# A gated branch in half units and a delta-rule pair projected early, in the first block of a two-block kernel

## The chip, the cores and the metric

One core of a Trainium2 chip runs the whole program in one launch. The metric is device time in microseconds (us), the median of the runs. Lower is better.

## The reference

Two transformer blocks act on 512 latent positions and 256 context positions of width 1024, batch 1, in float32. The change lies in the first block. There the normed and modulated input is projected by `w_in`, and the result feeds three branches:

- a pooling branch (4 windows);
- a delta-rule branch (RWKV, 6 heads of 64, two directions). A state is carried over the positions, context first, then latent positions:

```python
sa = einsum('bhvk,bhk->bhv', S, kk_t)
S = S * w_t - sa[..., None] * (kk_t * a_t) + v_t[..., None] * k_t
y = einsum('bhvk,bhk->bhv', S, r_t)
```

- a gated branch (HGRN, 6 heads of 64, two directions), a gated linear recurrence computed chunk by chunk, with `g` the running sum of the log of the forget gate within a chunk:

```python
o = (q * exp(g)) @ S + tril(sum_k q_t k_s exp(g_t - g_s)) @ i
S = exp(g_last) * S + (k * exp(g_last - g)).T @ i
```

The branches are concatenated, gated by a silu of another part of the projection, projected by `w_out`, and added to the input. The second block (a chunked delta net, attention, two feed-forward parts) isn't touched.

## The kernel before

The kernel is written in a tile language. Python traces the operations in program order; at build time a scheduler lays out each engine's fixed order, in which an operation that is ready may be put before earlier ones that are not. Tiles with the same tag share a number of slots (`bufs`); a new tile waits until the slot's last user is done. PSUM has 8 banks, split by tag in `banks(...)`.

**Projections.** `dense` (line 267) multiplies a 1024x128 block of weights with the input. Weights come in two halves of 512 rows by DMA (`wblock`, line 256): ACT rounds them into `whi` (line 263), VectorE (DVE) takes the rest into `wlo` (line 264), and TensorE (PE) makes three products per 128 rows (line 277). Streams have weight buffers of their own: "m" for the delta rule, gates and pooling, "f" for the gated branch, "a" for the `ada` vectors (line 307: 16 transfers each and matmuls of 128x256, line 318).

**The branch stage** is the second half of `block1` (from line 448), some 70 to 850 us of the trace. The PSUM banks are `mm` 2 (projections of stream "m" and the preparation), `rsc` 2 and `rch` 1 (delta rule), `mf` 2 (everything of the gated branch, its projections too) and `ma` 1 (ada). Two generators are advanced by turns in a loop of six steps (lines 472 to 481); each step also traces one of the six block-2 `ada` vectors, the first step a further one and the pooling branch.

**The delta rule** (`rwkv_pair`, line 615) goes over three pairs of heads. A pair projects k, v and r with a three-tap shift (`shift3`, line 588; eviction in lines 582 to 585), normalises keys into `kk`, and prepares decays and scaled keys (`rwkv_prep`: matmuls in line 689, tiles `tw`, `ta`, `G`, `km`, and the prepared keys BK in lines 724 and 727). Three groups of four chunks follow: `rwkv_pre` makes score matrices (line 763) and inverts triangles on DVE and PE; `rwkv_chunk` (line 914) passes the state on, chunk after chunk (lines 926 to 945; one of its matmuls is line 934); `rwkv_out` makes the output. A gate projection follows a group. After the third group a readout normalises y (lines 656 to 669).

**The gated branch** (`hgrn_pair`, line 983) has six units: three pairs of heads, two directions. A pair projects q and the values `it`; a unit projects z, from which come `g`, the keys, and the decayed keys `kd` (`hgrn_unit`, line 1042). Then six chunks are walked in order. The four latent chunks make scores at seven levels (`hgrn_levels`; 32-wide matmuls in lines 1084 to 1091), mask and sum the inner levels on DVE (1094, 1096), and copy the diagonal blocks and the outer levels into `sct` on ACT (1099 to 1104). Two matmuls a head with the state and with `sct` (1111, 1112) give the output. Between chunks the state is moved on: a transpose of `kd` on PE (1120), an ACT copy (1122), two matmuls (1125), and two DVE updates (1130) into a zeroed new tile `hS`.

Ahead of the gating at the end, `gated(j)` multiplies each branch's output with its gate on POOL and splits it (lines 484 to 491, 398, 399).

Of the kernel before, what the change touches and what calls it, by code (L numbers as in the profile page):

```python
# [49 lines left out]
def _consts():  # L50
    p = np.arange(128)
    c = {}
# [13 lines left out]
    for d in range(2):  # L66
# [9 lines left out]
        c[f"hgm{d}"] = np.concatenate(lv, 1) * 1.0  # L76
    s5, t5 = p[:, None] % 32, np.arange(32)[None]
# [120 lines left out]
class B:  # L198
    def __init__(self, ctx, tc, d, taps=()):
        self.tc, self.nc, self.d, self.taps = tc, tc.nc, d, taps  # L200
        self.ctx = ctx
        self.cst = ctx.enter_context(tc.tile_pool(name="cst", bufs=1))
        self.wp = ctx.enter_context(tc.tile_pool(name="wp", bufs=3))
        self.hp = ctx.enter_context(tc.tile_pool(name="hp", bufs=1))
        self.streams = {"m": (self.wp, 2, 2)}
        self.load_consts()
# [220 lines left out]
    def block1(self):  # L427
# [20 lines left out]
        with ExitStack() as ctx:  # L448
            ctx.enter_context(self.banks(mm=2, rsc=2, rch=1, mf=2, ma=1))
            ctx.enter_context(self.stream("f", 2, 1))  # L450
            ctx.enter_context(self.stream("a", 3, 1))
# [11 lines left out]
            self.sct = [self.f1.tile([128, 2, 128], F32, name=f"sct{a}") for a in range(2)]  # L463
            for x in self.sct:
                nc.gpsimd.memset(x, 0.0)
# [3 lines left out]
            rw = chain.from_iterable(self.rwkv_pair(p) for p in range(3))  # L469
            hg = chain.from_iterable(self.hgrn_pair(p) for p in range(3))  # L470
            next(rw)
            for n in range(6):
                for _ in range(2 - n % 2):
                    next(rw, None)
                next(hg)
                if n == 0:
                    self.ada(s, 0, d["mod_w"], 1, 2, mod[:, 16:24], self.V("mod_b", 16, 8), "a")
                    self.pool_branch()
                l, g = divmod(n, 3)
                self.ada(s, 2, d["ada_w"][l], g, 4, self.m2[l][:, 16 * g:16 * g + 16],  # L480
                         self.V("ada_b_2", 48 * l + 16 * g, 16), "a")
# [59 lines left out]
    def pool_branch(self):  # L541
        nc = self.nc
        for j in range(2):
# [23 lines left out]
            pw = self.f2.tile([128, 128], F32, tag="hkt", name="pw")  # L567
# [47 lines left out]
    def rwkv_pair(self, p):  # L615
        nc = self.nc
        k = self.f1.tile([128, NT], F32, name="rk")
        v = self.f1.tile([128, NT], F32, name="rv")
        r = self.f1.tile([128, NL], F32, name="rr")
        kk = self.f1.tile([128, NT], F32, name="rkk")  # L620
        self.shift3(5 + p, (LAT, CTX), k)
        self.shift3(8 + p, (LAT, CTX), v)
        self.shift3(2 + p, (LAT,), r, -256)
        nc.scalar.activation(kk, k, AF.Copy, scale=self.V("rwkv_k_k", p))
        sq = self.f1.tile([128, NT], F32, tag="tw", name="kksq")
        nc.gpsimd.tensor_tensor(sq, kk, kk, op=ALU.mult)
        rn = self.f1.tile([128, NT], F32, tag="G", name="kkrn")
        pieces = []
        for c0, cn in (LAT, CTX):
            o = self.mm()  # L630
            nc.tensor.matmul(o[:, :cn], self.C("bones"), sq[:, c0:c0 + cn], start=True, stop=True)
            pieces.append((rn[:, c0:c0 + cn], o[:, :cn]))
        self.rsqrt_bc(rn, pieces, 1.0, 3)
        nc.vector.tensor_tensor(kk, kk, rn, op=ALU.mult)
        pb = self.f1.tile([128, NL], F32, name="rpb")
        bk, ec = self.rwkv_prep(p, r, k, v, kk, pb)
        yield
        y = self.f1.tile([128, NL], F32, name="ry")
        st = self.f1.tile([128, 2, 64], F32, tag="rS", name="rS", bufs=8)
        nc.gpsimd.memset(st, 0.0)  # L640
        for g in range(3):
            pre = self.rwkv_pre(g, bk, v)
            sts = []
            for i in range(4):
                sts.append(st)
                st = self.rwkv_chunk(g, i, ec[:, :, 4 * g + i], pre, st)
            if g:
                self.rwkv_out(g, sts, pre, y)
            if 3 * p + g < 8:
                self.gate(3 * p + g)  # L650
            if g < 2:
                yield

        def readout():

            sq = self.f1.tile([128, NL], F32, name="rsq")
# [10 lines left out]
            if p < 2:  # L667
                nc.sync.dma_start(self.ymix[:, 2 + p], y)

        readout()  # L670

    def rwkv_prep(self, p, r, k, v, kk, pb):
# [70 lines left out]
    def rwkv_pre(self, g, bks, v):  # L743
# [49 lines left out]
        w = f1.tile([128, 8, 32], F32, tag="rw16", name="rw32")  # L793
# [28 lines left out]
    def inv8(self, c32, U):  # L822
# [29 lines left out]
        w = tl("w16", 32)  # L852
# [61 lines left out]
    def rwkv_chunk(self, g, i, ec, pre, st):  # L914
# [14 lines left out]
        xs = self.f1.tile([128, 128], F32, name="xs", bufs=2)  # L929
# [10 lines left out]
        st2 = self.f1.tile([128, 2, 64], F32, tag="rS", name="rS", bufs=8)  # L940
# [42 lines left out]
    def hgrn_pair(self, p):  # L983
        nc = self.nc
        f1, f2 = self.f1, self.f2
# [7 lines left out]
        for c0, n in ((2, 4), (0, 2)):  # L993
            tp = self.psum("mf", (128, 4, 128))
# [3 lines left out]
        oa = f1.tile([128, NL], F32, name="hoa")  # L998
        for dd in range(2):
            z = f1.tile([128, NT], F32, name="hz")  # L1000
            for (c0, cn), o in zip((LAT, CTX), self.dense(self.d["w_in"], 19 + 3 * dd + p, self.hh, self.hl, (LAT, CTX), st="f")):
                nc.scalar.copy(z[:, c0:c0 + cn], o[:, :cn])
            self.hgrn_unit(p, dd, q, it, z, oa)
            yield
# [776 lines left out]
```

## Time and profile before

| | us |
|---|---|
| median of 3 runs | 2729.93 (2725.15 to 2731.68) |
| profiled execution | 2736.78 |
| its span, first to last instruction | 2735.0 |
| PE busy in the span | 2523.7 |
| DVE busy | 1621.3 |
| ACT busy | 1276.9 |
| POOL busy | 319.3 |

PE is the matmul engine, PEld its weight loads, which overlap. A row of a window gives start and end, the length, then for PE, PEld, DVE, ACT and POOL the busy us with the number of instructions, then the mean granted clock of PE (1.00 is 2.4 GHz, 0.50 is 1.2 GHz), the share of DMA in use and GB/s. A window filtered by line or tile shows only engines that such instructions run on. Idle time of PE is length less busy time. A row of a group gives line, engine, operation, output and inputs, shapes and count, then busy us and mean ns of one, then the engine's idle time just before them and what ended it. A row of a wait reads: who waited, for whom, us in all, times, longest.

### The profile page before, as it was taken

The page shows a single profiled execution, that of the slowest core. Times are in us where ns is not written, and L with a number is a line of the kernel's source. Part 1 is how long each engine was busy: PE and PEld are TensorE (multiplying, and loading weights), DVE is VectorE, ACT ScalarE, POOL GpSimd, SP SyncE. Part 2 cuts the span into 40 slices and gives each one's busy share as a digit, 9 for nine tenths or more (in the row PEclk, how much of TensorE's full clock was granted, in tenths as well). Part 3 has the DMA queues.
Part 4 walks back from the last instruction along what each step waited for, and adds up shares of the span by engine and source line. Part 5 has one row for each costly group of instructions (what it writes and reads, how often), then busy time and mean ns, then how long its engine had stood idle before and what let it go on. Part 6 is the DMA issues. An engine that isn't in the chain of part 4 may idle for free.

```text
span 2735.0 us, 53289 instructions
## 1 busy us (share of the span) xinstructions
PE 2523.7 (92%) x21320; PEld 1990.5 (73%) x21320; DVE 1621.3 (59%) x3815; ACT 1276.9 (47%) x2840; POOL 319.3 (12%) x432
## 2 busy tenths in 40 slices
PE   7989979979877989989899999999998999999998
PEld 3655646545546777777677888888886888888888
DVE  4566574576565656777856443344463767664665
ACT  3454454545455656556434332233344555542444
POOL 0121121122112000111110110011000000010010
PEclk9999989989887999999989999999998999999999
DMA  6233432434334211111231112212231102233325
GB/s 206 77 94 118 139 98 92 125 100 134 93 104 146 72 39 32 36 41 37 65 105 47 62 63 64 63 63 66 80 105 44 32 27 95 78 100 93 100 89 157
DMA packets 159016, 231.10 MB, mean 84 GB/s; under 512 B 12976, under 2 KB 90032, under 8 KB 158768
## 3 DMA queue, kind: packets, MB, share of 16 engines
q1 hardware_dynamic: 158768, 227.70, 26.7%
q8 instruction: 167, 2.74, 0.4%
q14 instruction: 81, 0.66, 0.1%
HBM read 217.95 MB, written 9.70 MB: 83 GB/s over the span
## 4 chain that ended last, share of the span: by engine, by line
PE 47%; DVE 2%; ACT 2%; issue 1%; POOL 1%; DMA 0%; POOLq 0%; SPq 0%; DVEq 0%; ACTq 0%
PE mm L277 39%; PE ms L1735 2%; PE mt L1754 1%; PE mv L351 1%; PE mt L1748 1%; PE mm L1685 1%; PE mf L277 0%; DVE hl L423 0%; DVE ht L421 0%; POOL qr L1669 0%; ACT hh L422 0%; DMA raw<-mla_w_out 0%; ACT whi L263 0%; ACT qrh L1705 0%; PE mm L1665 0%
## 5 line engine op out<-in xcount | busy, mean ns | idle before, releaser
L264 DVE TENSOR_TENSOR wlo<-raw,whi 128x512 fp32r<-128x512 f32 (+3 forms) x560 | 391.3, 701 | 395.1 <-ACT whi L263 236.6
L263 ACT CAST whi<-raw 128x512 fp32r<-128x512 f32 (+3 forms) x560 | 331.9, 594 | 462.8 <-PE mm L277 398.9
L277 PE MATMUL mm<-hh,whi 128*128 128x512 f32 (+1 forms) x1960 | 483.8, 360 | 28.0 <-ACT hh L422 13.6
L277 PE MATMUL mm<-hl,whi 128*128 128x512 f32 (+1 forms) x1960 | 457.3, 350 | 0.0
L277 PE MATMUL mm<-hh,wlo 128*128 128x512 f32 (+1 forms) x1960 | 455.3, 350 | 0.4 <-DVE wlo L264 0.4
L277 PEld LDWEIGHTS mm<-hh,whi 128*128 128x128 f32 x1960 | 332.4, 192 | 89.7 <-ACT hh L422 21.0
L277 PEld LDWEIGHTS mm<-hl,whi 128*128 128x128 f32 x1960 | 329.7, 193 | 46.8 <-issue 3.6
L277 PEld LDWEIGHTS mm<-hh,wlo 128*128 128x128 f32 x1960 | 328.9, 193 | 45.0 <-issue 2.0
L1233 POOL TENSOR_TENSOR fc<-fc,fc 128x768 f32<-128x768 f32 (+1 forms) x44 | 69.2, 1573 | 867.9 <-DVE fc L585 625.8
L277 PE MATMUL mm<-fh,whi 128*128 128x256 f32 (+1 forms) x616 | 136.3, 340 | 1.0 <-ACT fh L398 1.0
L583 DVE SCALAR_TENSOR_TENSOR fc<-mm,vec,fc 128x511 f32<-128x511 f32 (+1 forms) x132 | 86.8, 658 | 80.7 <-ACT fc L582 80.7
L277 PE MATMUL mm<-fl,whi 128*128 128x256 f32 (+1 forms) x616 | 130.5, 330 | 0.0
L277 PE MATMUL mm<-fh,wlo 128*128 128x256 f32 (+1 forms) x616 | 129.3, 328 | 0.0
L582 ACT ACTIVATE fc<-mm,vec 128x512 f32<-128x512 f32 (+1 forms) x132 | 81.4, 617 | 97.2 <-PE mm L277 97.2
L277 PEld LDWEIGHTS mm<-fh,whi 128*128 128x128 f32 x616 | 99.8, 190 | 15.8 <-issue 3.4
L318 PE MATMUL ma<-raw,cvs 128*32 128x256 f32 x832 | 95.6, 427 | 15.3 <-DMA raw<-ada_w 10.6
L277 PE MATMUL mf<-hh,whi 128*128 128x512 f32 (+1 forms) x360 | 103.6, 387 | 6.0 <-ACT whi L263 3.4
L277 PEld LDWEIGHTS mm<-fl,whi 128*128 128x128 f32 x616 | 99.0, 190 | 11.3 <-issue 0.5
L1197 DVE SCALAR_TENSOR_TENSOR xr<-mm,m,xr 128x512 f32<-128x512 f32 (+1 forms) x112 | 66.5, 597 | 67.0 <-PE mm L277 66.8
L277 PEld LDWEIGHTS mm<-fh,wlo 128*128 128x128 f32 x616 | 98.6, 190 | 10.4
L351 PE MATMUL mv<-sq,con 128*128 128x256 f32 (+1 forms) x240 | 84.3, 452 | 12.4 <-ACT sq L355 12.0
L277 PE MATMUL mf<-hl,whi 128*128 128x512 f32 (+1 forms) x360 | 95.4, 367 | 0.0
(545 smaller groups left out, 4383.6 us busy)
## 6 DMA issues: line engine op xcount, KB each, us to landing
raw<-ada_w SPq DMA_DIRECT2D x96, 512.0 KB, 4.6
raw<-ffn_up SPq DMA_DIRECT2D x176, 256.0 KB, 2.8
raw<-ffn_down SPq DMA_DIRECT2D x96, 256.0 KB, 2.7
raw<-w_in SPq DMA_DIRECT2D x66, 256.0 KB, 2.9
raw<-ab_w_in SPq DMA_DIRECT2D x50, 256.0 KB, 2.6
raw<-ffn_down SPq DMA_DIRECT2D x48, 192.0 KB, 2.4
raw<-mod_w SPq DMA_DIRECT2D x16, 512.0 KB, 7.6
raw<-w_out SPq DMA_DIRECT2D x32, 256.0 KB, 2.9
```

Source lines behind the costliest of these rows:

```text
L263: nc.scalar.copy(hi[:, :nk], raw[:, :nk])
L264: nc.vector.tensor_tensor(lo[:, :nk], raw[:, :nk], hi[:, :nk].bitcast(F32), op=ALU.subtract)
L277: nc.tensor.matmul(o, a[:, k], b[:, k0 + k, t:e], start=(k0 == 0 and j == 0 and k == 0), stop=(k0 + n == nk and j == 2 and k == n - 1))
L318: nc.tensor.matmul(acc[32 * b:32 * b + 32, c:c + 256], s[:, k, :], t[:, b], start=(k == 0), stop=(k == 7))
L351: self.nc.tensor.matmul(v[:, :x.shape[1]], self.C("ones"), x, start=(k == 0), stop=(k == 7))
L582: nc.scalar.activation(out[:, c0:c0 + cn], o[:, :cn], AF.Copy, scale=w[1])
L583: nc.vector.scalar_tensor_tensor(out[:, c0 + 1:c0 + cn], o[:, :cn - 1], w[0], out[:, c0 + 1:c0 + cn], op0=ALU.mult, op1=ALU.add)
L1197: nc.vector.scalar_tensor_tensor(x, o[:, :cn], gcol(m, 0 if c0 else 1), x, op0=ALU.mult, op1=ALU.add)
L1233: nc.gpsimd.tensor_tensor(g, g, u, op=ALU.mult)
L1685: nc.tensor.matmul(o[:, e], a[:, k, T], b[:, k], start=(i == 0), stop=(i == 5))
L1735: nc.tensor.matmul(o[:, at:at + cn], a, b, start=(j == 0), stop=(j == 4))
L1748: nc.tensor.transpose(tp[:, j], p[:, (c0 + j) * 128:(c0 + j + 1) * 128], self.C("ident"))
```

## The change

The two generators become `rwkv_steps` and `hgrn_steps`, advanced in nine steps, one per group of the delta rule. The gated branch yields after each half of a unit (two latent chunks). All states of a unit are made at once by `hgrn_states` into a persistent tile `hS` of four states; `hgrn_prep` makes z, g and the transposed decayed keys `kt` one unit ahead. k and r of the next pair (`rwkv_load`) are traced after the second group, v (`rwkv_value`) and the preparation after the third. The mask of the diagonal blocks becomes one POOL product with a constant `b32`. PSUM tag `mf` becomes `hb`, used by the gated branch without its projections, which now use `mm`. Some buffer counts change.

```diff
-        self.streams = {"m": (self.wp, 2, 2)}
+        self.streams = {"m": (self.wp, 3, 2)}
...
-            ctx.enter_context(self.banks(mm=2, rsc=2, rch=1, mf=2, ma=1))
+            ctx.enter_context(self.banks(mm=2, rsc=2, rch=1, hb=2, ma=1))
             ctx.enter_context(self.stream("f", 2, 1))
-            ctx.enter_context(self.stream("a", 3, 1))
+            ctx.enter_context(self.stream("a", 2, 1))
...
-            for n in range(6):
-                for _ in range(2 - n % 2):
-                    next(rw, None)
-                next(hg)
+            for n in range(9):
+                next(rw, None)
+                for _ in range(1 + (n % 3 == 2)):
+                    next(hg, None)
                 if n == 0:
...
+                if n < 7:
+                    adas[n]()
...
+    def rwkv_steps(self):
+        now = self.rwkv_load(0)
+        v = self.rwkv_value(0)
+        for p in range(3):
+            bk, ec = self.rwkv_prep(p, *now, v, pb)
+            yield
...
+            for g in range(3):
+                pre = self.rwkv_pre(g, bk, v)
...
+                if g < 2:
+                    self.gate(3 * p + g)
+                    if g and p < 2:
+                        now = self.rwkv_load(p + 1)
+                    yield
+            if p < 2:
+                self.gate(3 * p + 2)
+                v = self.rwkv_value(p + 1)
...
-            sq = self.f1.tile([128, NL], F32, name="rsq")
+            sq = self.f1.tile([128, NT], F32, tag="km", name="rsq")[:, :NL]
...
-        w = f1.tile([128, 8, 32], F32, tag="rw16", name="rw32")
+        w = f1.tile([128, 8, 32], F32, tag="rc32", name="rw32")
...
-        xs = self.f1.tile([128, 128], F32, name="xs", bufs=2)
+        xs = self.f1.tile([128, 128], F32, name="xs")
...
-        st2 = self.f1.tile([128, 2, 64], F32, tag="rS", name="rS", bufs=8)
+        st2 = self.f1.tile([128, 2, 64], F32, tag="rS", name="rS", bufs=6)
...
+    def hgrn_steps(self):
+        q, it = self.hgrn_load(0)
+        prep = self.hgrn_prep(0, 0)
+        yield
+        for p in range(3):
+            oa = f1.tile([128, NL], F32, name="hoa")
+            for dd in range(2):
+                k, g, ge, kt = prep
+                self.hgrn_states(dd, ge, kt, it)
+                if dd == 0:
+                    prep = self.hgrn_prep(p, 1)
+                elif p < 2:
+                    prep = self.hgrn_prep(p + 1, 0)
+                for m in range(2):
+                    self.hgrn_chunks(dd, m, q, it, k, g, oa)
+                    if m == 0 or dd == 0:
+                        yield
...
+            if p < 2:
+                nc.sync.dma_start(self.ymix[:, 5 + p], oa)
+                q, it = self.hgrn_load(p + 1)
+            yield
...
+    def hgrn_prep(self, p, dd):
+        z = f1.tile([128, NT], F32, name="hz", bufs=2)
...
+        g = f1.tile([128, 6, 128], F32, name="hg", bufs=2)
...
+        for n0 in (0, 4):
+            n = min(4, 5 - n0)
+            tp = self.psum("hb", (128, 4, 128))
+            for n_ in range(n):
+                nc.tensor.transpose(tp[:, n_], kd[:, order[n0 + n_]], self.C("ident"))
+            nc.scalar.copy(kt[:, n0:n0 + n], tp[:, :n])
+        return z, g, ge, kt
+
+    def hgrn_states(self, dd, ge, kt, it):
+        kv = self.psum("hb", (128, 5, 64))
+        for n in range(5):
+            for h in range(2):
+                H = slice(64 * h, 64 * h + 64)
+                nc.tensor.matmul(kv[H, n], kt[:, n, H], it[:, order[n], H], start=True, stop=True)
+        ks = self.f1.tile([128, 5, 64], F32, name="hkv")
+        nc.scalar.copy(ks, kv)
+        for n in range(1, 5):
+            for h in range(2):
+                H = slice(64 * h, 64 * h + 64)
+                last = ks[H, 0] if n == 1 else self.hs[H, n - 2, H]
+                nc.vector.scalar_tensor_tensor(self.hs[H, n - 1, H], last, ge[H, order[n]:order[n] + 1], ks[H, n],
+                                               op0=ALU.mult, op1=ALU.add)
...
-                    for i in range(4):
-                        R = slice(32 * i, 32 * i + 32)
-                        nc.scalar.copy(sct[R, h, R], rd[R])
+                nc.gpsimd.tensor_tensor(sct[h].rearrange("p (i t) -> p i t", t=32),
+                                        rd.rearrange("p (o t) -> p o t", o=1).broadcast_to([128, 4, 32]),
+                                        self.C("b32").rearrange("p (i o) -> p i o", o=1).broadcast_to([128, 4, 32]), op=ALU.mult)
```

## Rows read from the trace of the kernel before

**Rows 1.** Busy time of the page: us, share of the span, instructions, by engine.

```profile
PE 2523.7 (92%) x21320; PEld 1990.5 (73%) x21320; DVE 1621.3 (59%) x3815; ACT 1276.9 (47%) x2840; POOL 319.3 (12%) x432
```

**Rows 2.** Windows of the branch stage: busy us by engine, clock, DMA share, GB/s.

```profile
187.00:240.00 53.00, 43.41 (x956) 29.06 (x956) 41.62 (x147) 33.04 (x123) 10.24 (x24) 0.81 0.28 86
...
306.00:336.00 30.00, 28.55 (x180) 21.39 (x181) 21.72 (x50) 19.51 (x47) 4.26 (x4) 1.00 0.35 111
336.00:378.00 42.00, 28.18 (x357) 14.78 (x351) 36.84 (x80) 20.53 (x51) 14.49 (x30) 0.72 0.46 148
...
434.00:473.00 39.00, 38.32 (x664) 27.89 (x662) 19.71 (x64) 18.73 (x47) 5.96 (x11) 1.00 0.31 98
473.00:552.00 79.00, 73.56 (x1286) 46.90 (x1284) 46.56 (x151) 41.57 (x152) 14.13 (x26) 0.91 0.41 128
...
566.00:608.00 42.00, 27.39 (x152) 15.54 (x152) 35.32 (x70) 22.57 (x37) 15.22 (x27) 0.75 0.35 113
...
674.00:717.00 43.00, 40.81 (x633) 29.25 (x629) 18.93 (x63) 16.21 (x43) 6.03 (x11) 0.92 0.22 73
717.00:798.00 81.00, 68.19 (x1304) 42.05 (x1300) 48.17 (x152) 44.43 (x159) 9.60 (x21) 0.89 0.40 125
...
808.00:849.00 41.00, 21.43 (x405) 12.18 (x405) 22.60 (x66) 20.33 (x86) 9.64 (x13) 0.50 0.38 123
sum 697.00, PE 595.02 PEld 381.76 DVE 421.90 ACT 352.11 POOL 131.79; mean PE 39.67 PEld 25.45 DVE 28.13 ACT 23.47 POOL 8.79
```

**Rows 3.** Windows of line 1084 alone, PE and PEld.

```profile
482.00:520.00 38.00, 5.71 (x384) 4.45 (x384) 0.89 0.55 170
```

**Rows 4.** Windows of line 934 alone, PE and PEld.

```profile
482.00:520.00 38.00, 0.00 (x0) 0.00 (x0) 0.89 0.55 170
```

**Rows 5.** Waits of PE, 70 to 850 us: total us, times, longest.

```profile
PE rsc L763 <- DVE BK L727: 18.3, 4, 7.7
PE mf L1112 <- ACT sct L1099: 11.0, 18, 2.7
PE ma L318 <- DMA raw<-ada_w: 10.6, 14, 2.8
PE mf L1111 <- ACT sct L1104: 8.6, 8, 2.2
```

**Rows 6.** Groups by line, ACT, 70 to 850 us.

```profile
L1099 ACT COPY sct<-hrd 32x32 f32<-32x32 f32 x192 | 41.1, 214 | 7.5 <-DVE hrd L1096 3.0 <-DVE rpr L847 0.6
...
L1122 ACT COPY hkt<-mf 128x128 f32<-128x128 f32 x30 | 7.5, 267 | 3.8 <-PE mf L1120 3.3
```

**Rows 7.** Groups by line, DVE, 70 to 850 us.

```profile
L1130 DVE SCALAR_TENSOR_TENSOR hS<-hS,hge,mf 64x64 f32<-64x64 f32 x60 | 16.8, 280 | 14.7 <-PE mf L1125 3.6 <-ACT hoa L1115 3.5 <-ACT hlv L1037 2.9
...
L583 DVE SCALAR_TENSOR_TENSOR rv<-mm,vec,rv 128x511 f32<-128x511 f32 (+1 forms) x6 | 3.7, 612 | 4.0 <-ACT rv L582 4.0
```

**Rows 8.** Groups by line, POOL, 70 to 850 us.

```profile
L1107 POOL TENSOR_TENSOR hqe<-hqe,hq 128x128 f32<-128x128 f32 x24 | 14.4, 602 | 72.8 <-ACT hqe L1106 60.5 <-PE ma L318 8.8 <-PE rsc L787 3.1
```

**Rows 9.** Timeline of ACT: start, length, instruction.

```profile
534.91 0.69 ACT L582 ACTIVATE rk<-mm,vec 128x512 f32<-128x512 f32 x1
```

**Rows 10.** Groups by line and shape, PE, 70 to 850 us.

```profile
L318 PE MATMUL ma<-raw,cvs 128*32 128x256 f32 x832 | 95.6, 427 | 15.3 <-DMA raw<-ada_w 10.6 <-DMA raw<-mod_w 2.9 <-ACT sct L1099 1.6
...
L277 PE MATMUL mf<-hh,whi 128*128 128x512 f32 x96 | 35.8, 463 | 0.5 <-ACT whi L263 0.5
```

**Rows 11.** DMA issues, 70 to 850 us: count, KB each, us to landing.

```profile
raw<-ada_w SPq DMA_DIRECT2D x96, 512.0 KB, 4.6
```

**Rows 12.** Timeline of POOL and DVE, 815 to 830 us.

```profile
816.18 1.27 POOL L490 TENSOR_TENSOR gb<-ga,gb 128x512 f32<-128x512 f32 x1
...
816.76 1.24 DVE L399 TENSOR_TENSOR hl<-gb,hh 128x512 fp32r<-128x512 f32 x1 [0.26 <-ACT hh L398]
...
828.88 0.68 DVE L399 TENSOR_TENSOR hl<-gb,hh 128x512 fp32r<-128x512 f32 x1
```

**Rows 13.** Windows of the matmuls into tile mf, PE alone.

```profile
434.00:473.00 39.00, 19.46 (x89) 1.00 0.31 98
```

More of the change, by code (lines that the diff above doesn't have):

```diff
@@ L76, in _consts @@
         c[f"hgm{d}"] = np.concatenate(lv, 1) * 1.0
+    c["b32"] = (p[:, None] // 32 == np.arange(4)[None]) * 1.0
     s5, t5 = p[:, None] % 32, np.arange(32)[None]
@@ L462, in block1 @@
                 nc.gpsimd.memset(a, 0.0)
-            self.sct = [self.f1.tile([128, 2, 128], F32, name=f"sct{a}") for a in range(2)]
-            for x in self.sct:
-                nc.gpsimd.memset(x, 0.0)
+            self.hs = self.f1.tile([128, 4, 128], F32, name="hS")
+            nc.gpsimd.memset(self.hs, 0.0)
             self.rwkv_lora()
@@ L566, in pool_branch @@
             nc.vector.tensor_tensor(tot, tot, u, op=ALU.subtract)
-            pw = self.f2.tile([128, 128], F32, tag="hkt", name="pw")
+            pw = self.f2.tile([128, 128], F32, tag="hqe", name="pw", bufs=1)
             nc.gpsimd.memset(pw, 0.0)
@@ L668, in readout, with rwkv_value, rwkv_load, rwkv_prep @@
                 nc.sync.dma_start(self.ymix[:, 2 + p], y)
-        readout()
-    def rwkv_prep(self, p, r, k, v, kk, pb):
+                y = self.f1.tile([128, NL], F32, name="ry")
+    def rwkv_value(self, p):
+        v = self.f1.tile([128, NT], F32, name="rv")
+        self.shift3(8 + p, (LAT, CTX), v)
+        return v
+    def rwkv_load(self, p):
+        nc = self.nc
+        k = self.f1.tile([128, NT], F32, name="rk")
+        r = self.f1.tile([128, NL], F32, name="rr")
+        kk = self.f1.tile([128, NT], F32, name="rkk")
+        self.shift3(5 + p, (LAT, CTX), k)
+        nc.scalar.activation(kk, k, AF.Copy, scale=self.V("rwkv_k_k", p))
+        sq = self.f1.tile([128, NT], F32, tag="tw", name="kksq")
+        nc.gpsimd.tensor_tensor(sq, kk, kk, op=ALU.mult)
+        rn = self.f1.tile([128, NT], F32, tag="G", name="kkrn")
+        pieces = []
+        for c0, cn in (LAT, CTX):
+            o = self.mm()
+            nc.tensor.matmul(o[:, :cn], self.C("bones"), sq[:, c0:c0 + cn], start=True, stop=True)
+            pieces.append((rn[:, c0:c0 + cn], o[:, :cn]))
+        self.rsqrt_bc(rn, pieces, 1.0, 3)
+        nc.vector.tensor_tensor(kk, kk, rn, op=ALU.mult)
+        self.shift3(2 + p, (LAT,), r, -256)
+        return r, k, kk
+    def rwkv_prep(self, p, r, k, kk, v, pb):
         nc = self.nc
@@ L997, in hgrn_pair @@
             nc.scalar.copy(it[:, c0:c0 + n], tp[:, :n])
[L998 to L1004, printed above, removed]
-        sq = f1.tile([128, NT], F32, tag="htmp", name="osq")
@@ L1006, in hgrn_pair @@
-        nc.gpsimd.tensor_tensor(sq[:, :NL], oa, oa, op=ALU.mult)
-        va = self.psum("mf")
-        nc.tensor.matmul(va, self.C("bones"), sq[:, :NL], start=True, stop=True)
-        rs = f1.tile([128, NT], F32, tag="hg", name="ors")
-        self.rsqrt_bc(rs[:, :NL], [(rs[:, :NL], va)], 1.0 / 64, 1)
-        nc.vector.scalar_tensor_tensor(oa, oa, self.V("hgrn_norm_g", p), rs[:, :NL], op0=ALU.mult, op1=ALU.mult)
-        self.last[5 + p] = oa
-        if p < 2:
-            nc.sync.dma_start(self.ymix[:, 5 + p], oa)
+        return q, it
```

234 lines of the change are left out of this document (104 added, 130 removed).

## The prediction, made before the changed kernel was run

> **What bounds the kernel now.** I read the page's busy line first: TensorE (PE) is busy for 92% of the span [rows 1], so a change to one stage can gain only where PE in that stage stands idle or runs at its lower clock. The change touches the branch stage alone, some 70 to 850 us. Next I read the windows table of that stage [rows 2]. Over 152 to 849 us PE is busy 595.0 of 697 us, so 102 us are idle. It is uneven. Two stretches, 434 to 473 and 674 to 717, in which a group of the delta rule runs beside filler, leave 0.7 and 2.2 us idle at a granted clock of 1.00 and 0.92. The idle time is in four kinds of stretch: 187 to 240 and 717 to 798 (9.6 and 12.8 us idle, each holding a unit of the gated branch), 336 to 378 and 566 to 608 (13.8 and 14.6 us; keys of the next pair are prepared and VectorE, DVE, is busy 36.8 and 35.3 of 42 us), and the end, 808 to 849 (19.6 us of 41, clock 0.50, so all of it at the lower of PE's two levels, 1.2 GHz).
>
> Third, two windows tables of one line each. The score matmuls of the gated branch come in bursts: all 384 of a unit lie within 482 to 520 [rows 3]. In the same window the delta rule's chunk matmuls stand at zero [rows 4]. So a gated unit, traced as one block, displaces a group: the group in 473 to 552 lasts 79 us and the one in 717 to 798 lasts 81, while the undisturbed ones last 39 and 43 [rows 2]. That is no loss by itself, since the displaced work is not lost, but it makes the thin stretches and leaves the last unit alone at the end.
>
> Fourth, the waits of PE within 70 to 850 us [rows 5]: for BK (line 727, the prepared keys) 18.3 us, for `sct` (the masked scores, lines 1099 and 1104) 11.0 and 8.6, for ada weights by DMA 10.6.
>
> **The change part by part.** Measured by the profiled execution, 2736.78 us around a span of 2735.0; it stands 6.85 us above the median of the runs, 2729.93.
>
> *The state chain.* Before, each of five chunks in a unit makes a transpose, an ACT copy (267 ns, [rows 6]), two matmuls and two DVE updates of 280 ns reading PSUM [rows 7], between the outputs of chunks, in the two `mf` banks that the scores and the projections also use. After, five transposes come at once, two wide ACT copies in place of five, ten matmuls into one bank, one ACT copy, and eight DVE updates in SBUF. PE's instructions are the same in number. DVE loses 12 of 60 updates (12 x 0.28 = 3.4 us), the memsets of the states go, and one of six exponentials and products of `kd` a unit. None of these lies on PE; what counts is that the score, output and state steps no longer take turns in a bank.
>
> *The score mask.* Before, four ACT copies a head put the diagonal blocks in place: 192 x 214 ns = 41.1 us of ACT [rows 6], and PE waits 11.0 + 8.6 = 19.6 us for the result. After, one POOL product of 128x128 a head, 48 in all, in front of the three other ACT copies. The nearest POOL row is `hqe`, 128x128, 602 ns [rows 8]: 48 x 0.60 = 29 us on POOL, which is busy 319 of 2735 us [rows 1], in a chain where 4 x 0.214 = 0.86 us of ACT stood. The chain gets 0.26 us shorter a head, and three copies now wait for POOL's semaphore too; behind them on ACT wait the weight casts of line 263. The wait of PE can go from 19.6 to somewhere between 10 and 25 us; I take 13.
>
> *Bursts broken up.* Units are split in two halves, one per group, and the next unit's z, g and kt are made one unit ahead. For 187 to 240 and 717 to 798: idle 9.6 + 12.8 = 22.4 us. With the score wait I take 10 of it, and 5 for the clock (0.81 and 0.89 there). **Gain 15, bounds 0 and 27.**
>
> *The end.* Unit 5's scores now lie beside the last group instead of behind it. Of 808 to 849, 19.6 us are idle, and the 21.4 us of PE work at clock 0.50 would take at best 10.7 at 1.00: 30 us at most. But the last step is thin after the change too: the ada transfers and gates are handed out by the step before or earlier, and the closing norm and gating stay. **Gain 20, bounds 5 and 30.**
>
> *k and r of the next pair ahead of the last group.* The projections themselves are PE work and move, they don't go: 306 to 336 has PE busy 28.6 of 30 us. What can go is the start of the preparation behind them. 336 to 378 and 566 to 608 hold 28.4 us idle, and at clocks 0.72 and 0.75 half or more of 84 us at the lower level, worth up to 15 us of PE's 55.6. Two things hold it back: preparation is bound by DVE there, and its `km` now shares a slot with the readout's `rsq`, so that half waits for the readout. Also, the order is already looked ahead at compile time: for pair 2, k is evicted at 534.9 us, before the readout that ends that pair near 552 [rows 9]. **Gain 15 of 43, bounds 0 and 35.**
>
> *One pair of banks for all projections.* The gated projections lose `mf` and join the delta rule's in `mm` (two banks), handed out in program order. Before, 12 calls of the gated branch filled PE from banks of their own (96 matmuls of one of six forms alone take 35.8 us, [rows 10]). Now each waits for the eviction of the call before: an ACT operation and two DVE operations of 612 ns each where it is a shift [rows 7], some 1.8 us. 12 x 1.8 = 22 us if nothing covers it. PE's cover is the ada matmuls (95.6 us in all, [rows 10]), scores and groups. If that cover is gone, it's 22 us; if a bank is held for a value tile that isn't free, more (the slow rival). **Loss 5, bounds 0 and 22.**
>
> *ada with two buffers in place of three, weights with three in place of two.* Bytes and transfers are equal. An ada transfer lands in 4.6 us [rows 11]; one fewer in flight makes PE's 10.6 us wait at most half as long again, and SP, an in-order queue, stands longer before an ada issue with weight loads behind it. The third weight buffer lets one load go ahead of it. **Loss 4, bounds -3 and 10.**
>
> *POOL against DVE.* When POOL multiplied 512 columns (816.18, 1.27 us), the DVE subtraction that began in it took 1.24 us; the same one alone takes 0.68 [rows 12]. So a POOL product can hold a DVE operation until it ends. 48 new products of 0.6 us: up to 29 us on DVE, mostly where DVE has just finished the mask's reduction and isn't critical. **Loss 1, bounds 0 and 15.** The Trainium skill, SBUF — State Buffer, section Who interferes with whom, has this as a lock: a DVE instruction with two SBUF inputs contends with a POOL instruction that reads SBUF, and issue order decides who blocks. The trace agrees with its 1.24 against 0.68 us; by that rule, taken for every product, the loss term would be the 15 and not the 1.
>
> The state buffers from 8 to 6, `xs` from 2 to 1 and the shared `w` slot cost nothing as long as a group's chunks follow one another through the state, as they do; bound 3 us. The first steps and everything after 850 us stay.
>
> Sum: 15 + 20 + 15 - 5 - 4 - 1 = 40 us. 2736.8 - 40 = 2696.8 for a profiled execution, and 2730 - 40 = **2690** for the median.
>
> **Rivals.** *A: the units really interleave.* Then bursts no longer displace groups, and idle and clock losses go over the whole stage: 15 + 20 + 15 become 27 + 30 + 35 = 92, less 10: 2648. For it: groups without a unit run in 39 to 43 us with PE full [rows 2]. Against: what is moved only displaces filler, since PE is at 85% in the stage.
>
> *B: nothing to move.* The look-ahead already does it [rows 9], PE's work is unchanged, and gains of 10 are eaten by bank and buffer waits: 2722 to 2738.
>
> *C: the lock.* Every POOL product holds DVE in stretches where DVE is full: the loss of 15 in place of 1, and the score chain gains nothing (7 us less): 2730 - 40 + 14 + 7 = 2711. The page named above is its rule. Against it: 602 ns on POOL [rows 8] replace 856 on ACT, and PE waits for the sum of them.
>
> *D: slower, by the shared banks.* `rv` has one buffer, freed when the last group has transposed the old values. A value projection that runs early holds both `mm` banks until then; gates, the gated z and the next pair's preparation queue behind it, and PE has only ada, with two buffers. Each of the 12 gated calls then uncovers some 5 us: 60 - 40 = 20 us slower, 2750. It decides from 40 / 12 = 3.3 us per call. For it: in 434 to 473 half of PE's time, 19.46 of 39 us, is projections into just that second pair of banks [rows 13]. Against: 306 to 336 runs three projections back to back in the two `mm` banks with 1.5 us idle [rows 2].
>
> **How the numbers follow.** Forecast 0.42 (2675 to 2705), A 0.20, C 0.11, B 0.10, D 0.17. A measurement of this kernel tells 0.3%, 8 us, from no change. Faster: forecast, A and C, 0.73; same: B, 0.10; slower: D, 0.17. The time is the likeliest case's, 2690. The range: A's low end with the bounds' best sum is 2640; at the top it takes in C, B and the near half of D, 2742. About 2 in 10 lie outside, half of them in D.
>
> **What would show it.** Right: the window of the last unit's scores overlaps the last group's chunk matmuls, and the low-clock stretch at the end is under 25 us (41 before); score matmuls of a unit come in two halves; PE's wait for `sct` is near 13 us; the stretch around the next pair's preparation has under 10 us idle; the branch stage ends near 806 instead of 846. Wrong: PE idle before line 277 or the preparation's line 689 on evictions in `mm` above 20 us (D); DVE two-input operations of 128x128 twice as long beside `sct` on POOL (C); a stage that ends within 8 us of before (B). If the end of the stage stays and later stages move, my reading that they don't change is wrong.

## The result: slower, and where the time went

The changed kernel takes 2756.07 us (median of 4 runs, 2755.01 to 2767.82) against 2730.8 us for the kernel before on the same chip: ratio 1.0104, 95% interval [1.0071, 1.0137]. The forecast was 2690 with a range to 2742. It was wrong in sign, and the time lies near rival D's 2750. An experiment's ratio below is always to the kernel before, run beside it, with its 95% interval; 0.1% is 2.7 us. One of the ten executions of after_mf took 5890 us and is left out of its ratio.

The busy line of the page after answers to [rows 1]: us, share of the span, instructions.

```profile
PE 2508.2 (91%) x21320; PEld 1993.4 (72%) x21320; DVE 1618.4 (59%) x3806; ACT 1233.9 (45%) x2630; POOL 321.7 (12%) x443
```

ACT lost 43 us, near the 41.1 reckoned from 192 copies of 214 ns [rows 6], and PE has the same number of instructions. The kernel is slower although PE, DVE and ACT are busy for less time, and PEld and POOL for only 2 to 3 us more. The traces date the loss by the first matmul of each pair's readout (line 647; 658 before) and by PE's first matmul of block 2 (line 352; 351 before), in us:

| kernel | 1st readout | 2nd | 3rd | block 2 |
|---|---|---|---|---|
| before | 306.4 | 552.4 | 799.4 | 849.1 |
| after | 350.1 | 593.2 | 830.9 | 868.7 |
| after_rk | 349.8 | 599.0 | 843.4 | 852.9 |
| after_mf | 327.6 | 570.2 | 798.7 | 838.5 |
| mf_rk | 325.0 | 569.3 | 809.0 | 819.5 |
| mf_rk_act | 322.0 | 562.6 | 796.8 | 807.9 |
| before_mm | 317.1 | 584.2 | 838.0 | 870.8 |

After the change the first pair is 43.7 us late. The next two take 243.1 and 237.6 us, where they took 246.0 and 247.0. Block 2 begins 19.7 us late, and from there to the end of the span 1884.5 us pass (1885.9 before). So the change acts inside the branch stage only, and the lateness arises in the first pair.

Two cautions belong to this table. Each trace is one execution: before_km and before_a2 below, which take as long as the kernel before, have their first readout at 303.9 and 300.7 us and block 2 at 844.2 and 836.1, so a difference of some 10 us in it proves nothing by itself. And the 43.7 us are not all loss: mf_rk, which is faster than the kernel before, is 18.5 us late there too, with more work of PE ahead of that readout (235.1 us busy from 70 us on, 214.0 before), since gated work has moved forward.

Windows of the kernel after, from the first preparation to block 2 (columns as in [rows 2]):

```profile
110.00:150.00 40.00, 24.90 (x117) 10.31 (x116) 31.54 (x65) 15.56 (x22) 8.71 (x13) 0.65 0.42 128
150.00:178.00 28.00, 27.95 (x148) 23.22 (x147) 11.28 (x41) 8.69 (x18) 3.47 (x5) 0.96 0.18 53
...
350.00:364.00 14.00, 8.86 (x40) 2.24 (x40) 7.48 (x12) 3.62 (x5) 1.85 (x4) 0.76 0.57 172
364.00:400.00 36.00, 29.70 (x158) 20.20 (x159) 29.25 (x79) 13.14 (x24) 8.07 (x13) 0.76 0.40 124
...
593.00:640.00 47.00, 31.63 (x170) 14.77 (x169) 35.82 (x76) 16.55 (x25) 14.02 (x19) 0.67 0.54 168
...
831.00:869.00 38.00, 2.36 (x5) 0.71 (x6) 6.98 (x11) 5.13 (x10) 12.37 (x11) 0.55 0.46 153
```

The same first two windows of the kernel before, which the prediction did not read:

```profile
110.00:150.00 40.00, 35.33 (x160) 20.76 (x159) 32.77 (x63) 19.03 (x30) 14.22 (x26) 0.91 0.29 90
150.00:178.00 28.00, 25.21 (x448) 18.16 (x447) 13.52 (x49) 11.65 (x31) 3.87 (x6) 1.00 0.14 44
```

Two places stand out. From 110 to 150 us PE is busy 24.9 us instead of 35.3, at a granted clock of 0.65 instead of 0.91. From 831 to 869 it is busy 2.4 of 38 us. The stretches between a readout and the end of the next preparation (350 to 400, 593 to 640) are idle for 11.4 and 15.4 us, where those of [rows 2] had 13.8 and 14.6.

**The first place.** Windows of the dense matmuls alone, PE and PEld, in the same two stretches. Before (line 277):

```profile
110.00:150.00 40.00, 15.49 (x70) 11.67 (x69) 0.91 0.29 90
150.00:178.00 28.00, 17.22 (x62) 10.62 (x63) 1.00 0.14 44
```

After (line 278):

```profile
110.00:150.00 40.00, 1.98 (x15) 1.70 (x13) 0.65 0.42 128
150.00:178.00 28.00, 24.33 (x120) 19.29 (x120) 0.96 0.18 53
```

PE's timeline after, where they come:

```profile
152.11 1.20 PE L748 MATMUL mm<-rpb,con 128*128 128x512 f32 x2
152.74 1.48 PE L278 MATMUL mm<-hh,whi 128*128 128x512 f32 x4
...
177.16 0.65 PE L278 MATMUL mm<-hh,wlo 128*128 128x256 f32 x4
177.65 0.49 PE L801 MATMUL rsc<-con,rv 128*128 128x128 f32 x3
178.07 0.75 PE L875 MATMUL rsc<-rt,ro 32*32 32x32 f32 x64
178.81 0.33 PE L940 MATMUL rch<-uv,scs 128*64 128x64 f32 x2
```

Line 748 is the preparation's last use of `mm`. The gated projections, traced behind it, begin 0.63 us later and run back to back to 178 us. While the preparation ran on DVE (busy 31.5 of 40 us) and left PE idle, none of them could start; when the first group was ready, they stood in front of its inversion (line 875) and its first chunk (line 940).

**The second place.** Timeline after, all engines, from the last readout on:

```profile
832.79 1.04 POOL L649 TENSOR_TENSOR rsq<-ry 128x512 f32<-128x512 f32 x1 [5.57 <-DVE ry L648]
...
837.27 0.32 SPq L490 DMA_DIRECT2D gb<-ygate  x1
...
838.11 1.26 POOL L491 TENSOR_TENSOR gb<-ry,gb 128x512 f32<-128x512 f32 x1 [4.29 <-DVE ry L654]
...
845.76 1.26 POOL L491 TENSOR_TENSOR gb<-ga,gb 128x512 f32<-128x512 f32 x1 [4.46 <-DMA gb<-ygate]
...
851.55 1.26 POOL L491 TENSOR_TENSOR gb<-ga,gb 128x512 f32<-128x512 f32 x1 [4.53 <-DMA gb<-ygate]
...
855.10 0.61 SPq L504 DMA_DIRECT2D xr<-x  x1
...
857.50 1.26 POOL L491 TENSOR_TENSOR gb<-hoa,gb 128x512 f32<-128x512 f32 x1 [4.69 <-DMA gb<-ygate]
...
868.75 1.22 PE L352 MATMUL mv<-sq,con 128*128 128x256 f32 x2 [33.74 <-ACT sq L356]
```

In `gated(j)` every second gate tile `gb` is taken from the tag `km`, and `rsq` of the last readout now is too. So those products wait for the readout, and then go one after the other through the slot: load the gate, multiply, round, take the rest, nearly 6 us a turn. The wait of SP (its queue issues the loads; 780 to 870 us) for the readout to give the slot back (line 653, the last to read `rsq`):

```profile
SPq L490 <- DVE ry L653: 43.4, 1, 43.4
```

Behind these loads in SP's queue stand those of `xr` for the next norm, issued at 855.10. PE stands for 33.7 us.

PE's waits after, 70 to 870 us, answer to [rows 5]:

```profile
PE ma L319 <- DMA raw<-ada_w: 41.4, 29, 3.3
PE mv L352 <- ACT sq L356: 33.7, 1, 33.7
...
PE hb L1181 <- ACT sct L1174: 5.2, 5, 2.2
...
PE hb L1181 <- POOL sct L1167: 2.4, 3, 1.0
...
PE rsc L777 <- DVE BK L741: 2.2, 1, 2.2
...
PE hb L1182 <- ACT sct L1174: 2.1, 6, 0.7
```

The waits that the change aims at did shrink: `sct` from 19.6 to 9.7 us, BK from 18.3 to 2.2. (Whether the mask did it is asked below, at before_pool.)

### The profile page after: what moved, and what is told of

It is laid out like the page before. It is cut to its first block, busy times and chain, and to the rows that moved or that the text cites. A ratio compares the mean times of both kernels' runs of the same rounds, so it can differ in the third digit from the quotient of the medians.

```text
span 2753.2 us, 53004 instructions
## 1 busy us (share of the span) xinstructions
PE 2508.2 (91%) x21320; PEld 1993.4 (72%) x21320; DVE 1618.4 (59%) x3806; ACT 1233.9 (45%) x2630; POOL 321.7 (12%) x443
## 4 chain that ended last, share of the span: by engine, by line
PE 47%; DVE 2%; ACT 1%; POOL 1%; issue 1%; DMA 0%; POOLq 0%; DVEq 0%; ACTq 0%
PE mm L278 39%; PE ms L1791 2%; PE mt L1810 1%; PE mv L352 1%; PE mt L1804 1%; PE mm L1741 1%; PE mf L278 0%; DVE ht L422 0%; DVE hl L424 0%; POOL qr L1725 0%; POOL qr L1724 0%; ACT qrh L1761 0%; PE mm L1721 0%; ACT hh L423 0%; ACT whi L264 0%
## 5 line engine op out<-in xcount | busy, mean ns | idle before, releaser
L278 PE MATMUL mm<-hh,whi 128*128 128x512 f32 (+1 forms) x2128 | 527.2, 362 | 21.4 <-ACT hh L423 12.2
L278 PE MATMUL mm<-hl,whi 128*128 128x512 f32 (+1 forms) x2128 | 499.4, 351 | 0.0
L278 PE MATMUL mm<-hh,wlo 128*128 128x512 f32 (+1 forms) x2128 | 493.7, 349 | 1.2 <-DVE wlo L265 1.1
L278 PEld LDWEIGHTS mm<-hh,whi 128*128 128x128 f32 x2128 | 361.8, 193 | 92.2 <-ACT hh L423 19.7
L278 PEld LDWEIGHTS mm<-hl,whi 128*128 128x128 f32 x2128 | 358.2, 193 | 50.9 <-issue 2.9
L278 PEld LDWEIGHTS mm<-hh,wlo 128*128 128x128 f32 x2128 | 355.6, 193 | 50.4 <-DVE wlo L265 3.3
L319 PE MATMUL ma<-raw,cvs 128*32 128x256 f32 x832 | 101.6, 468 | 51.4 <-DMA raw<-ada_w 41.4
L584 DVE SCALAR_TENSOR_TENSOR fc<-mm,vec,fc 128x511 f32<-128x511 f32 (+1 forms) x132 | 86.8, 658 | 80.7 <-ACT fc L583 80.6
L352 PE MATMUL mv<-sq,con 128*128 128x256 f32 (+1 forms) x240 | 84.5, 452 | 41.1 <-ACT sq L356 40.7
L278 PEld LDWEIGHTS mm<-fh,wlo 128*128 128x128 f32 x616 | 98.6, 190 | 10.5
L319 PEld LDWEIGHTS ma<-raw,cvs 128*32 128x32 f32 x832 | 25.0, 119 | 97.9 <-DMA raw<-ada_w 60.7
L586 DVE SCALAR_TENSOR_TENSOR fc<-mm,vec,fc 128x511 f32<-128x511 f32 (+1 forms) x132 | 86.9, 658 | 3.1
```

Source lines behind the costliest of these rows:

```text
L278: nc.tensor.matmul(o, a[:, k], b[:, k0 + k, t:e], start=(k0 == 0 and j == 0 and k == 0), stop=(k0 + n == nk and j == 2 and k == n - 1))
L319: nc.tensor.matmul(acc[32 * b:32 * b + 32, c:c + 256], s[:, k, :], t[:, b], start=(k == 0), stop=(k == 7))
L352: self.nc.tensor.matmul(v[:, :x.shape[1]], self.C("ones"), x, start=(k == 0), stop=(k == 7))
L584: nc.vector.scalar_tensor_tensor(out[:, c0 + 1:c0 + cn], o[:, :cn - 1], w[0], out[:, c0 + 1:c0 + cn], op0=ALU.mult, op1=ALU.add)
L586: nc.vector.scalar_tensor_tensor(out[:, c0:c0 + cn - 1], o[:, 1:cn], w[2], out[:, c0:c0 + cn - 1], op0=ALU.mult, op1=ALU.add)
```

## The experiments

**The two places, one at a time and together.** after_rk gives the last readout's `rsq` another slot; after_mf gives the gated projections back the banks of the gated scores; mf_rk does both.

```diff
-            sq = self.f1.tile([128, NT], F32, tag="km", name="rsq")[:, :NL]
+            sq = self.f1.tile([128, NT], F32, tag="rk" if p == 2 else "km", name="rsq")[:, :NL]
```

> The changed kernel, except that the last pair's readout takes its scratch rsq from the slot of rk, free since the last preparation, and not from km. Theory T (the end): in the changed kernel the gate loads of j = 1, 3, 5 and 7 share the slot km with rsq, so they run one after another behind the last readout, 838 to 859 us, and SP issues the loads of xr behind them; PE stands from 832 to 869 us. With rsq elsewhere these loads go ahead of the readout, the branch stage ends within 12 us of it, near 847, and the time is 2756 - 20 = 2736 us (2728 to 2742). Rivals: if the lost time lies in the shared banks, in the start order or in the ada buffers (theories D, S, A), the end only waits for something else and the time stays within 6 us of 2756.

Measured: 2738.74 us, 1.0030 [1.0014, 1.0047], 17 us less than after. PE's wait ahead of block 2 falls to 5.4 us:

```profile
PE mv L352 <- ACT sq L356: 5.4, 1, 5.4
```

POOL's timeline shows the last readout and a single gate product behind it:

```profile
845.30 1.04 POOL L649 TENSOR_TENSOR rsq<-ry 128x512 f32<-128x512 f32 x1 [5.57 <-DVE ry L648]
850.63 1.26 POOL L491 TENSOR_TENSOR gb<-ry,gb 128x512 f32<-128x512 f32 x1 [4.28 <-DVE ry L654]
```

```diff
-            ctx.enter_context(self.banks(mm=2, rsc=2, rch=1, hb=2, ma=1))
+            ctx.enter_context(self.banks(mm=2, rsc=2, rch=1, mf=2, ma=1))
...
-            va = self.psum("hb")
+            va = self.psum("mf")
```

(and so at every `psum("hb")`; a projection of stream "f" takes `mf` where that tag exists, else `mm`)

> The changed kernel, except that the projections of the gated branch go back to the two banks that the gated branch's scores use, as before the change. Theory D (shared banks): in 110 to 150 us they again fill PE beside the first preparation, the first chunk of the delta rule comes at some 155 to 160 us and not at 180, and the time falls by 15 to 30 us, to 2726 to 2741. Theory S (start order) gives a part of this, since the order in which they are traced stays. Rivals: by theories T and A, under 6 us gained; and if scores and projections hold each other up in two banks, as the change supposes, slower than 2756 by up to 20.

Measured: 2721.5 us, 0.9971 [0.9953, 0.9989], 35 us less than after. Its window of the dense matmuls has them back in the preparation:

```profile
110.00:150.00 40.00, 19.71 (x96) 15.55 (x94) 0.90 0.19 60
```

Both together:

> Both repairs in the changed kernel: the gated branch's projections in the banks of its scores, and the last readout's scratch out of km. They cost at different places (theory D in 110 to 180 us, theory T behind the last readout), so if both hold the gains add: 35 + 17 under the changed kernel, 2700 to 2710 us, and the stage ends within 20 us of the last readout. Rival: the repaired end is covered by the gated unit or by the load of xr, and the second repair gives under 8 us: 2714 to 2722.

Measured: 2702.21 us, 0.9915 [0.9896, 0.9933]. So the slot is worth 15 us on top of the banks (0.9971 to 0.9915) and 20 without that repair (1.0104 to 1.0030), the banks 31 to 36. With both repaired, what is left of the change gains 0.85%, 23 us.

**The same two edits alone, in the kernel before.** before_mm moves only the gated projections to `mm`.

```diff
-            ctx.enter_context(self.banks(mm=2, rsc=2, rch=1, mf=2, ma=1))
+            ctx.enter_context(self.banks(mm=2, rsc=2, rch=1, hb=2, ma=1))
...
-                    sc = self.psum("mf")
+                    sc = self.psum("hb")
```

(and so at the gated branch's other banks, but not its projections)

> The kernel before, with the gated branch's projections moved to the two banks of the delta rule's projections and nothing else. Theory D, as a property of the banks and not of the new order: PE idles in 110 to 150 us, the first readout comes 20 us later or more, and the time rises by 20 to 40 us, to 2750 to 2770. Rival: in the old order units and groups alternate anyway, so that the projections seldom meet: within 8 us of 2730.

Measured: 2759.34 us, 1.0130 [1.0106, 1.0153], a loss of 35 us. Its first window of the dense matmuls (line 277) is as empty as that of after:

```profile
110.00:150.00 40.00, 2.06 (x7) 1.16 (x7) 0.66 0.42 131
```

So the shared banks cost this without any other part of the change. Here most of the delay arises in the second pair (1st readout 10.6 us late, 2nd 31.8); that part was not followed further, so for it the banks are shown as the cause, and the way they act is not.

before_km puts only `rsq` into the slot `km`.

```diff
-            sq = self.f1.tile([128, NL], F32, name="rsq")
+            sq = self.f1.tile([128, NT], F32, tag="km", name="rsq")[:, :NL]
```

> The kernel before with one change: the readout's rsq shares its slot with the preparation's km, and so with the gate tiles of the products at the end. Theory J: the shared slot costs only where no gated unit covers it; before, the last unit stands alone behind the last readout for some 40 us and covers the four gate products that queue behind the slot, so the time goes up by 0 to 6 us, 0.999 to 1.003. Rival: the slot's queue ends last whatever lies beside it, and it costs 15 to 20 us here as it did in the kernel after, 1.005 to 1.008.

Measured: 2731.8 us, 1.0011 [0.9997, 1.0025]: no difference that can be told. POOL's timeline there shows the gate products among the last unit's work:

```profile
815.74 1.30 POOL L490 TENSOR_TENSOR gb<-ry,gb 128x512 f32<-128x512 f32 x1 [3.62 <-DMA gb<-ygate]
...
818.00 0.55 POOL L1107 TENSOR_TENSOR hqe<-hqe,hq 128x128 f32<-128x128 f32 x1
825.83 0.45 POOL L1107 TENSOR_TENSOR hqe<-hqe,hq 128x128 f32<-128x128 f32 x1 [7.28 <-ACT hqe L1106]
826.24 1.27 POOL L490 TENSOR_TENSOR gb<-ga,gb 128x512 f32<-128x512 f32 x1
```

So in the old order the slot costs nothing that can be told, and in the new one 15 to 20 us: it costs when the unit that used to stand alone at the end, and covered the gating, is gone. The thin stretch that I wanted to remove was the cover of the next thing.

**Two explanations that fell.** after_order traces the first gated load and preparation behind the first group of the delta rule.

```diff
             next(rw)
-            next(hg)
...
-                for _ in range(1 + (n % 3 == 2)):
+                for _ in range(1 + (n == 0) + (n % 3 == 2)):
```

> The changed kernel, except that the gated branch's first projections are traced behind the first group of the delta rule and not ahead of it. Theory S (start order): the 25 us of projections at 152 to 178 us no longer stand ahead of the first group's inversion, the first readout comes at 320 to 335 us and not at 350, and the time falls by 10 to 25 us, to 2731 to 2746. Theory D: PE still idles in 120 to 150, and the projections come later by as much, so under 8 us gained. T and A: no change within 6 us.

Measured: 2761.19 us, 1.0108 [1.0089, 1.0128]. No gain: the first projections of the gated branch still hang on `mm`, and the first readout comes at 353.4 us (350.1 in after).

before_a2 takes one ada buffer away from the kernel before.

```diff
-            ctx.enter_context(self.stream("a", 3, 1))
+            ctx.enter_context(self.stream("a", 2, 1))
```

> The kernel before with two ada buffers in place of three, nothing else. Theory A (ada buffers): PE's wait for ada weights rises from 10.6 to some 40 us, as in the changed kernel (41.4), and the time rises by 12 to 30 us, to 2743 to 2760. T, D and S: within 6 us of 2730, since what PE waits for there it gets back elsewhere.

Measured: 2732.05 us, 1.0007 [0.9993, 1.0021], with this wait of PE:

```profile
PE ma L318 <- DMA raw<-ada_w: 27.5, 22, 3.2
```

The wait grew from 10.6 to 27.5 us and the time did not. The ada matmuls fill holes: where nothing else can run, the hole's end is put down to the transfer that the filler awaited. So the largest wait of after, 41.4 us, can't be read as what the ada buffers cost; with the projections back in their own banks it is 30.3 us in after_mf, so part of it is the first place under another name. The Trainium skill, Perfetto Trace Analysis, section Optimization Strategy, says to find the gaps of the limiting engine, see which semaphore ends them and make that start sooner; by that rule the ada transfers come first. The run disagrees: 17 us more of this very wait cost nothing that could be told.

**The other parts, undone one by one in the repaired kernel.** mf_rk_kr traces k and r of the next pair behind the last group again.

```diff
-                    if g and p < 2:
-                        now = self.rwkv_load(p + 1)
                     yield
             if p < 2:
                 self.gate(3 * p + 2)
+                now = self.rwkv_load(p + 1)
```

> As mf_rk, with k and r of the next pair traced behind the last group again, beside v. Theory K (as predicted, the early k and r gain 15 us): 10 to 20 us slower than mf_rk, in front of the second and third preparation. Rival L (the scheduler looked ahead anyway, and the preparation is bound by VectorE and waits for the readout): within 5 us of mf_rk.

Measured: 2707.88 us, 0.9936 [0.9918, 0.9955], 6 us more than mf_rk, with intervals that overlap.

mf_rk_act puts the score mask back on ACT.

```diff
+            for t in sct:
+                nc.gpsimd.memset(t, 0.0)
...
-                nc.gpsimd.tensor_tensor(sct[h].rearrange("p (i t) -> p i t", t=32),
...
+                for i in range(4):
+                    R = slice(32 * i, 32 * i + 32)
+                    nc.scalar.copy(sct[h][R, R], rd[R])
```

> As mf_rk, with the score mask undone: four ACT copies a head into a tile that POOL zeroes, in place of the POOL product. Theory M (the mask helps): ACT gets 41 us of copies back and PE's waits for the scores rise by 8 us or more: 5 to 15 us slower than mf_rk. Rival C (POOL holds DVE): the products go, DVE's two-input operations get shorter, and it is 0 to 10 us faster than mf_rk.

Measured: 2696.16 us, 0.9898 [0.9880, 0.9915], the fastest of all kernels here and 1% under the kernel before. Whether the mask itself costs these 5 us can't be told from overlapping intervals. So the mask was also put alone into the kernel before (before_pool):

```diff
-                    for i in range(4):
-                        R = slice(32 * i, 32 * i + 32)
-                        nc.scalar.copy(sct[R, h, R], rd[R])
+                    nc.gpsimd.tensor_tensor(sct[:, h].rearrange("p (i t) -> p i t", t=32),
...
```

> The kernel before with the score mask alone taken from the change: one POOL product of 128x128 a head in place of four ACT copies, 48 in all. Theory M: the mask saves ACT 41 us but lies on a chain that the matmul engine waits for anyway, and ACT isn't the bound; taken back in the repaired kernel it gave 6 us, so here it costs 0 to 8 us, 1.000 to 1.003. Rival N: the gain of 6 us that I took for the price of the mask is scatter, and the mask is worth what I forecast, a gain of some 6 us, 0.996 to 0.999.

Measured: 2717.75 us, 0.9960 [0.9943, 0.9977]. My theory M falls: alone the mask gains some 10 us, at the edge of what rival N gave. Its POOL group there, by shape:

```profile
L1098 POOL TENSOR_TENSOR sct<-hrd,con 128x128 f32<-128x128 f32 x48 | 22.1, 460 | 64.7 <-DVE hrd L1097 49.0 <-DVE rx L849 9.1 <-DVE m L328 3.7
```

A product takes 460 ns, not the 602 that I took from [rows 8]. But PE's wait for the masked scores did not get shorter there (70 to 850 us):

```profile
PE mf L1113 <- ACT sct L1105: 9.2, 11, 3.0
PE mf L1112 <- ACT sct L1105: 6.2, 4, 2.3
PE mf L1112 <- POOL sct L1098: 5.3, 5, 1.8
```

That is 20.7 us, against 19.6 in [rows 5]. And in mf_rk_act, with the mask on ACT again, the same waits are 10.3 us, as in mf_rk (10.5). So the wait fell with the new order, not with the mask, and where the mask's 10 us come from in before_pool, and why they are not seen in mf_rk, stays open.

mf_rk_act_whole undoes the half units, mf_rk_act_m2 the third weight buffer.

```diff
-                for _ in range(1 + (n % 3 == 2)):
+                if n % 3:
                     next(hg, None)
...
-                    if m == 0 or dd == 0:
-                        yield
+                if dd == 0:
+                    yield
```

> The best version so far (both repairs, the score mask back on ACT: 0.9898 of the kernel before) with the gated units traced whole again, two per pair behind the second and third group, so the split into halves is undone and nothing else. Theory H: the halves are what carries the 28 us that this version gains, since they spread the score matmuls over all groups; then undoing them gives 10 to 20 us back, 0.993 to 0.997, and the stretches with whole units in them get thin again. Rival I: the scheduler moves the units' work as filler anyway, and what carries the gain is that the states are made at once and z, g and kt one unit ahead; then the time stays within 5 us, 0.988 to 0.992.

Measured: 2702.34 us, 0.9906 [0.9884, 0.9928].

```diff
-        self.streams = {"m": (self.wp, 3, 2)}
+        self.streams = {"m": (self.wp, 2, 2)}
```

> The best version (both repairs, score mask on ACT: 0.9898 of the kernel before) with the delta rule's weight stream on two buffers again in place of three, the ada stream still on two: the one other part of the change that can be undone by a single number. Theory P: as with the ada buffers, a weight load that stands a little longer in the queue is covered by filler, so this costs 0 to 5 us, 0.989 to 0.993. Rival Q: the third buffer lets the projections run ahead and carries a good part of the 28 us; without it the time is 0.994 to 0.999.

Measured: 2702.21 us, 0.9903 [0.9885, 0.9921]. Neither can be told from 0.9898, so neither the halves nor the third buffer carries most of the 28 us of the best version, though either may be worth a few. What remains is the states made at once, z, g and kt one unit ahead, the gated branch's start ahead of the first group, and k and r early (6 us or none); the first three were not undone, so that they carry it is argued only.

## Why the prediction was wrong

**"One pair of banks for all projections. Loss 5, bounds 0 and 22"** is the step that failed. It measured 31 to 36 us, above its own upper bound. I priced the wait of each call on the eviction ahead of it, 12 x 1.8 us. The runs show a price of position: a bank of a tag goes to the next tile in program order, so projections traced behind a preparation cannot fill the preparation. Rival D had the queue, but laid it to a value tile held by `rv`, and expected PE to be seen idle before line 277 on evictions. That sign did not come; the row of after (PE, by shape) shows almost no idle time before these matmuls:

```profile
L278 PE MATMUL mm<-hh,whi 128*128 128x512 f32 x254 | 84.7, 445 | 0.2 <-ACT whi L264 0.2
```

Matmuls that are not yet allowed leave no wait of their own here. That D's time was nearly right is luck: it came about by another way than D's, and D's own sum is off, since the 40 that it starts from has the 5 for the banks taken off already (60 less 45 is 15, and 2745). The row I leaned on against D, three projections back to back in `mm`, told that two banks suffice for one producer, not that two producers may share them.

**"The end. Gain 20, bounds 5 and 30"** also failed. I named the slot shared by `km` and `rsq`, but only for the preparation, not for `gated`, which takes the same tag. The half of the step that could be seen came only in part. The last unit no longer stands behind the last group: 336 of its 384 score matmuls lie in 780 to 813 us (line 1153; windows of that line, PE and PEld),

```profile
780.00:813.00 33.00, 7.54 (x336) 5.76 (x336) 0.66 0.07 19
813.00:831.00 18.00, 0.00 (x0) 0.00 (x0) 0.86 0.01 2
```

but of the last group's 32 chunk matmuls (line 942) only 8 lie beside them, and the other 24 follow alone:

```profile
780.00:813.00 33.00, 0.64 (x8) 0.51 (x8) 0.66 0.07 19
813.00:831.00 18.00, 1.62 (x24) 1.33 (x24) 0.86 0.01 2
```

PE then stands for 33.7 us, and 15 to 20 us of that come back when the slot is freed. In mf_rk 10.5 us pass from the last readout to block 2, against 49.6 before, when the last unit's work stood there.

**The other terms.** k and r early: 15 forecast, about 6 measured with intervals that overlap, inside the bounds of 0 and 35. Ada buffers: 4 forecast, 2 measured and within the uncertainty. POOL against DVE: 1 forecast, and none seen in the sum: DVE is busy for 1621.9 us in the whole run of before_pool and for 1621.3 before. The Trainium skill, SBUF — State Buffer, section Who interferes with whom, taken for every product, made it 15; before_pool disagrees with that, by DVE's busy time and by the 10 us that the mask gained there. The score wait shrank to 9.7 us, under the 13 that I took, but not by the mask, to which I had put it. That the bursts' 15 came from halving the units isn't shown: undone, that moves 0.08%, well within the interval. Later stages did not move, as said.

Of the signs that I named for being right, the halves and the score wait came. The low-clock stretch at the end is 38 us long and not under 25, the stretches around the next preparations have 11.4 and 15.4 us idle and not under 10, and the stage ends near 869 us and not 806. At the low end of the range, the bounds' best sum is 27 + 30 + 35 + 3 = 95 us and 2635, not 2640.

The repaired parts together gain 23 us (28 with the mask on ACT), where the forecast without the term for the banks made 45. The sign was lost to the banks: with them alone repaired the kernel is faster than before (0.9971), with the slot alone repaired it is still slower (1.0030).

## What to carry to other kernels

When an edit lets two streams of work share a tag (a PSUM pair, a buffer slot), write down who asks for the tag in program order and what must be done before each may have it; the price is what the later one was meant to fill, not the eviction of the one ahead. Before a thin stretch at the end of a stage is removed, look for every use of what it covers, in the next stage too. And before a large wait is mended, ask whether the waiting work is filler: its wait names the hole, not the cause.

## What was not expected of the hardware

In the state chain I counted a saving of 12 updates of 280 ns on DVE. The updates of the kernel after, by shape:

```profile
L1104 DVE SCALAR_TENSOR_TENSOR hS<-hS,hge,hkv 64x64 f32<-64x64 f32 x36 | 14.3, 397 | 1.2
L1104 DVE SCALAR_TENSOR_TENSOR hS<-hkv,hge 64x64 f32<-64x64 f32 x12 | 3.3, 274 | 0.9 <-ACT hkv L1099 0.7
```

The 36 that read the state of the step before, beside the increment, take 397 ns in the mean; the 12 that read the increment's tile alone take 274, as the 280 of [rows 7] with the increment in PSUM. So 48 updates cost 17.6 us where 60 had cost 16.8, and the saving that I counted was none.

The mean hides what happens. The eight updates of a unit take 3.2 to 3.3 us in four units and 2.2 to 2.3 in the other two. One unit of each kind (windows of line 1104, DVE alone):

```profile
313.50:317.50 4.00, 3.22 (x8) 0.85 0.84 266
568.00:572.00 4.00, 2.20 (x8) 1.00 0.86 266
```

In each of the four a single update takes 1.30 to 1.36 us, and it begins within 0.1 us of the start of a 128x512 product of a gate on POOL. In the first of the two windows above:

```profile
315.62 1.27 POOL L539 TENSOR_TENSOR sg<-sg,se 128x512 f32<-128x512 f32 x1 [2.37 <-ACT se L340]
315.67 1.30 DVE L1104 SCALAR_TENSOR_TENSOR hS<-hS,hge,hkv 64x64 f32<-64x64 f32 x1
```

The update of the same chain just ahead of it took 0.28 us, and so did the one behind it. So it is not the chain from one update to the next: a DVE update with all its inputs in SBUF was held until POOL's product ended. Four such cases, 1 us each, ate the saving.
